# Projection matmuls given a scheduling offset of 200 in the first phase of a diffusion step on one core

## The chip, the core and the metric

The kernel runs on one core of one Trainium2 chip. The time is the device time of one execution in microseconds (us). The engines are TensorE (PE for its matmuls, PEld for its weight loads), VectorE (DVE), ScalarE (ACT), GpSimd (POOL) and SyncE (SP, which issues the DMAs). Each engine works through its own list of instructions in the order in which the program was built, and waits at an instruction whose inputs are not ready, even where a later one could run.

## The reference

One layer of a diffusion backbone is computed for a prompt of 128 tokens and a sample of 2048 tokens, model width 1024:

```
h = rmsnorm(x) * (1 + scale) + shift
p = h @ w_in                     # 1024 x 2832, one combined projection
A: gated DeltaNet (short conv on q/k/v, two scans in chunks of 64)
B: spatial gating MLP            C: average pooling minus identity
D: 2-D Fourier transform         each times silu(its gate columns of p)
out = x + gate * (concat(A, B, C, D) @ w_out);  y = rmsnorm(out)
```

All is float32. The outputs are y for the prompt and the sample and the prompt's final scan states.

## The kernel before

The 17 tiles of 128 tokens are worked on in three groups: group 0 has tiles 0 to 5, group 1 tiles 6 to 11, group 2 tiles 12 to 15 and the prompt's tile 16. The program has two phases.

**The first phase** is `phase_a`, called once for each group. For a group, `x_fin` transposes the normalised x on PE (L342, into the one PSUM buffer `pc`), ACT applies scale and shift (L344), and `h_split` writes the result as a high and a low half into `BIG` (L353 on DVE, L354 on DVE or POOL). All projections read these halves. The weights come in slices of 128 columns: `load_w` loads a slice by two DMAs (`wst`), ACT makes its high half (L242), DVE and POOL one part each of its low half (L243). There are three slots for slices. Then `mm3` makes one projection: 24 matmuls (8 slices of the contraction, three products of halves each) that add up in one of three PSUM buffers `pj`, all on L250. A slice of `w_in` is used for two chunks of tokens in the first phase, 384 and 392 wide in groups 0 and 1, 320 and 320 in group 2, so for 48 matmuls. The projections of the first phase are those of branch D with the beta and decay logits (272 columns), of C, and of q, k and v of two pairs of heads.

What follows on a projection in the first phase is a chain of small work: the short convolution (L842 on DVE), transposes back to token order (L642), the scalars of the decay (L562, L586, L587, L597), the products of k with k and of k with q (L673, L703), and, for a whole group, the `lanes`: transposes of the triangular blocks (L731), a solution in 30 steps, each a product and a sum on DVE (L741, L743), and its way back (L767, then L783, L784, L792 and L793). The records leave for DRAM. All these small matmuls are short, 10 to 64 columns or a 128x128 transpose.

**The second phase** begins after the third group (`Ring.late` is set to True): the gates' projections (L250 again, called by `gates`), branch B, the scan of 34 steps (L1053), the Fourier branch, and at the end the output projection of 17 tiles, 96 matmuls for every four column blocks.

**What sets the order.** The program is written in one sequence, and a scheduler then puts each engine's instructions in an order by a priority, which is the position in the sequence, among those that it takes to be ready. `hp(o)` opens a block whose instructions get a priority as if they stood o instructions earlier. The weight loads and `x_prep`, `x_fin` have 500 (`OW`, `OX`). The block in `mm3` has 0 (`OP`), so a projection competes by its own place in the sequence, behind all small matmuls written ahead of it:

```
def mm3(out, lh, rh, ks=range(KC), first=0, last=KC - 1):
    with hp(OP):
```

The engines' lists are fixed when the program is built; nothing is reordered at run time.

## Time and profile before

| | |
|---|---|
| median of 3 runs | 1208.77 us (1204.91 to 1215.5) |
| profiled execution | 1211.1 us, of it 1209.3 us from the first to the last instruction |
| mean granted TensorE clock | 0.952 |
| PE busy | 1090.1 us (90%) |
| PEld busy | 986.3 us (82%) |
| DVE busy | 815.1 us (67%) |
| POOL, ACT busy | 432.6 us (36%), 417.9 us (35%) |

The profile is of one execution. An engine counts as busy from the start to the modelled end of an instruction, so a busy PE is not a PE at its best rate. The clock column gives the share of 2.4 GHz that was granted to TensorE; it is 1.0 or 0.5 at any moment, and a mean in a longer stretch. In the trace, the 64-wide float32 products (L562, L586, L587, L673, L703, L767, L1053 and the like) appear as two matmuls for each one of the program; projections and transposes appear once.

### The profile page before, as it was taken

To read this page: it belongs to the slowest core of one execution; us is meant where nothing else is said; L and a number is where in the kernel's file an instruction comes from. 1 tells how busy PE (TensorE), PEld (TensorE's weight loads), DVE (VectorE), ACT (ScalarE), POOL (GpSimd) and SP (SyncE) were. 2 spreads that over 40 slices of the span, in tenths; PEclk is the share of its full clock that TensorE was granted. 3 is DMA by queue.
4 is the path that set the end of the run, shared out by engine and by line. 5 is a ranking of instruction groups with operands and counts; after the bars stand their busy time and mean duration, and the time that the engine had idled before them with its cause. 6 is when DMAs were issued, how large, how long until landed. Compare 5 with 4: busy or idle time off the path is not lost.

```text
span 1209.3 us, 29864 instructions
## 1 busy us (share of the span) xinstructions
PE 1090.1 (90%) x12211; PEld 986.3 (82%) x12211; DVE 815.1 (67%) x1864; ACT 417.9 (35%) x837; POOL 432.6 (36%) x429
## 2 busy tenths in 40 slices
PE   5888988998799698898979989898999889999997
PEld 2488977998779697875879888887899778999997
DVE  3666886799974699934884633784243488878665
ACT  2355667656565756123123111121111211111211
POOL 1347364726442237510231242232135343433212
PEclk9899998999879799898999999999999989999999
DMA  9879549943644564645264556589355645544331
GB/s 309 302 250 316 139 120 232 279 131 83 148 114 104 126 151 112 192 142 143 70 187 125 160 165 211 181 262 306 89 160 167 213 136 166 173 133 150 106 131 70
DMA packets 251391, 204.28 MB, mean 169 GB/s; under 512 B 109138, under 2 KB 218706, under 8 KB 250998
## 3 DMA queue, kind: packets, MB, share of 16 engines
q1 hardware_dynamic: 251254, 202.37, 56.7%
q8 instruction: 96, 1.57, 0.5%
q14 instruction: 41, 0.34, 0.1%
HBM read 138.86 MB, written 63.46 MB: 167 GB/s over the span
## 4 chain that ended last, share of the span: by engine, by line
PE 45%; DVE 17%; DMA 11%; issue 4%; ACT 3%; SPq 1%; POOL 1%; DVEq 0%; ACTq 0%; POOLq 0%
PE pj L250 34%; PE pa L1053 3%; DMA wst<-in_wt_dram 2%; DVE LL L743 2%; DVE ltmp L741 2%; DVE BIG L243 2%; DVE acc L842 1%; DMA X<-xd_d 1%; DMA ada<-in_ada_dram 1%; PE pb L1295 1%; DMA hr<-h_d 1%; DMA wos<-in_wo_dram 1%; DVE BIG L240 1%; DMA wst<-in_wv_dram 1%; PE pb L1393 1%
## 5 line engine op out<-in xcount | busy, mean ns | idle before, releaser
L250 PE MATMUL pj<-BIG 128*128 128x256 f32 (+4 forms) x3888 | 615.9, 313 | 16.7 <-ACT g L1222 4.0
L250 PEld LDWEIGHTS pj<-BIG 128*128 128x128 f32 x3888 | 560.9, 195 | 36.2 <-issue 10.8
L250 PE MATMUL pj<-BIG,yh 128*128 128x256 f32 x1088 | 197.5, 286 | 3.6 <-ACT BIG L1355 2.4
L243 POOL TENSOR_TENSOR BIG<-wst,BIG 128x512 fp32r<-128x512 f32 (+1 forms) x66 | 96.0, 1455 | 235.4 <-DVE BIG L240 137.3
L250 PEld LDWEIGHTS pj<-BIG,yh 128*128 128x128 f32 x1088 | 164.6, 190 | 7.0 <-ACT BIG L1355 2.6
L250 PE MATMUL pj<-BIG,yl 128*128 128x256 f32 x544 | 141.3, 284 | 0.0
L250 PEld LDWEIGHTS pj<-BIG,yl 128*128 128x128 f32 x544 | 98.7, 190 | 0.7
L240 DVE CAST BIG<-wst 128x512 fp32r<-128x512 f32 (+2 forms) x72 | 38.6, 540 | 74.8 <-DMA wst<-in_wt_dram 34.5
L1060 POOL TENSOR_TENSOR gS<-S,sc_s 128x256 f32<-128x256 f32 x32 | 20.9, 655 | 133.8 <-DVE S L1075 128.3
L842 DVE SCALAR_TENSOR_TENSOR acc<-raw,prm,acc 128x768 f32<-128x768 f32 (+1 forms) x72 | 64.2, 908 | 5.5 <-ACT acc L840 5.5
L1374 ACT ACTIVATE yh<-yt 128x768 fp32r<-128x768 f32 (+1 forms) x34 | 20.7, 629 | 128.9 <-issue 47.3
L1222 ACT ACTIVATE g<-pj 128x256 f32<-128x256 f32 (+1 forms) x64 | 23.3, 396 | 118.3 <-PE pj L250 111.8
L243 DVE TENSOR_TENSOR BIG<-wst,BIG 128x512 fp32r<-128x512 f32 (+1 forms) x66 | 53.4, 808 | 15.9 <-ACT BIG L242 13.8
L1413 POOL TENSOR_TENSOR z<-z,xs 128x1024 f32<-128x1024 f32 x16 | 41.8, 2612 | 57.1 <-DVE z L1405 52.0
L741 DVE TENSOR_TENSOR ltmp<-LL 128x60 f32<-128x60 f32 (+14 forms) x90 | 53.6, 595 | 4.5 <-ACT LL L734 3.1
L743 DVE TENSOR_TENSOR LL<-LL,ltmp 128x60 f32<-128x60 f32 (+14 forms) x90 | 55.3, 614 | 1.4
L242 ACT ACTIVATE BIG<-wst 128x512 fp32r<-128x512 f32 (+1 forms) x60 | 37.6, 632 | 35.3 <-DMA wst<-in_wt_dram 14.0
L354 POOL TENSOR_TENSOR BIG<-h,BIG 128x384 fp32r<-128x384 f32 (+2 forms) x28 | 26.7, 953 | 54.0 <-DVE BIG L353 37.4
L1075 DVE TENSOR_TENSOR S<-pa,gS 128x256 f32<-128x256 f32 x34 | 14.3, 420 | 42.1 <-PE pc L1053 35.0
L1375 DVE TENSOR_TENSOR yl<-yt,yh 128x768 fp32r<-128x768 f32 (+1 forms) x34 | 37.3, 1112 | 7.8 <-ACT yh L1374 7.8
L1405 DVE TENSOR_TENSOR z<-pj,gbc 128x256 f32<-128x256 f32 x68 | 26.0, 419 | 22.5 <-PE pj L250 22.2
L1071 ACT ACTIVATE xn<-pa 128x256 f32<-128x256 f32 x34 | 12.9, 381 | 80.8 <-PE pa L1053 73.2
(291 smaller groups left out, 1846.1 us busy)
## 6 DMA issues: line engine op xcount, KB each, us to landing
wst<-in_wt_dram SPq DMA_DIRECT2D x96, 256.0 KB, 3.5
R<-rec_d SPq DMA_DIRECT2D x136, 128.0 KB, 3.1
ada<-in_ada_dram SPq DMA_DIRECT2D x24, 512.0 KB, 5.3
C<-com_d SPq DMA_DIRECT2D x68, 128.0 KB, 3.1
xs<-xs_d SPq DMA_DIRECT2D x16, 512.0 KB
out_dram<-z SPq DMA_DIRECT2D x16, 512.0 KB, 3.1
x<-in_xs_dram SPq DMA_DIRECT2D x13, 512.0 KB
xs_d<-x SPq DMA_DIRECT2D x13, 512.0 KB, 6.1
```

What stands on the lines that cost most here:

```text
L240: nc.vector.tensor_copy(hi[:, ks, a:a + w], st[:, :, :w])
L242: nc.scalar.activation(hi[:, ks, a:a + w], st[:, :, :w], AF.Copy)
L243: (nc.vector if k0 == 0 else nc.gpsimd).tensor_tensor(lo[:, ks, a:a + w], st[:, :, :w], hi[:, ks, a:a + w].bitcast(F32), op=ALU.subtract)
L250: nc.tensor.matmul(out, lh[a](k), rh[b](k), start=(k == first and i == 0), stop=(k == last and i == 2))
L354: (nc.gpsimd if f % 2 else nc.vector).tensor_tensor(hT[1][:, f, off:off + w], h, hi.bitcast(F32), op=ALU.subtract)
L741: nc.vector.tensor_tensor(tv, X[:, :, j, j + 1:32].unsqueeze(2).to_broadcast([128, 2, j, ni]), bc(X[:, :, 0:j, j], ni), op=ALU.mult)
L743: nc.vector.tensor_tensor(X[:, :, 0:j, j + 1:32], X[:, :, 0:j, j + 1:32], tv, op=ALU.add)
L842: nc.vector.scalar_tensor_tensor(o, raw[:, si + j:si + j + n], w[:, j:j + 1], o, op0=ALU.mult, op1=ALU.add)
L1053: nc.tensor.matmul(ps[o, q], lh(q)[hp], rh[hp, q])
L1375: nc.vector.tensor_tensor(yl[:, q], yt[:, q], yh[:, q].bitcast(F32), op=ALU.subtract)
L1405: nc.vector.tensor_tensor(z[:, ns], ps, gbc[:, cd, ns], op=ALU.mult)
L1413: nc.gpsimd.tensor_tensor(z, z, xs, op=ALU.add)
```

## The change

The block in `mm3` gets 200 in the first phase, and 0 as before in the second. A projection matmul that the scheduler takes to be ready then goes ahead of any small matmul that is written up to 200 instructions ahead of it. The instructions themselves, the tiles, the buffers and the weight loads are the same; x_fin keeps its 500 and so stands ahead of the projections still.

```diff
-    OW, OX, OP = 500, 500, 0
+    OW, OX = 500, 500
...
     def mm3(out, lh, rh, ks=range(KC), first=0, last=KC - 1):
-        with hp(OP):
+        with hp(0 if Ring.late else 200):
```

Three places of PE's list show what moves. The first is in group 1, where the 48 products of k with k of one pair of heads stand (L673); `pj` is a projection, `pb` the PSUM buffers of the small matmuls. Before:

```order
L642 MATMUL pb<-cm,acc 128x128 x6
L250 MATMUL pj<-BIG 128x272 x105
L673 MATMUL pb<-sl 32x64 x48
L250 MATMUL pj<-BIG 128x384 x7
L250 MATMUL pj<-BIG 128x392
```

The same kind of products in the changed kernel, again in group 1:

```order
L673 MATMUL pb<-sl 32x64
L250 MATMUL pj<-BIG 128x392
L673 MATMUL pb<-sl 32x64 x23
L250 MATMUL pj<-BIG 128x384
L673 MATMUL pb<-sl 32x64
L250 MATMUL pj<-BIG 128x384
L673 MATMUL pb<-sl 32x64
L342 MATMUL pc<-cm,x 128x128
```

One closed block of 48 has become runs that alternate with single projection matmuls.

The second place is the beginning of group 2, while its x is still being transposed (L342). 272-column projections are the first of the group; 320-column ones are its chunks of C, q, k and v; L767 is the way back of the lanes of group 0. Before:

```order
L250 MATMUL pj<-BIG 128x272 x2
L767 MATMUL pa<-cm,LL 64x48 x9
L597 MATMUL pb<-cm,kt 24x128
L642 MATMUL pb<-cm,sl 128x128 x4
L250 MATMUL pj<-BIG 128x272 x3
L767 MATMUL pa<-cm,LL 64x48
L250 MATMUL pj<-BIG 128x272
L767 MATMUL pa<-cm,LL 64x48 x2
L342 MATMUL pc<-cm,x 128x128
L767 MATMUL pa<-cm,LL 64x48 x5
```

In the changed kernel:

```order
L250 MATMUL pj<-BIG 128x272 x2
L250 MATMUL pj<-BIG 128x320 x19
L342 MATMUL pc<-cm,x 128x128
L250 MATMUL pj<-BIG 128x320 x5
L250 MATMUL pj<-BIG 128x272 x7
L597 MATMUL pb<-cm,kt 24x128
L642 MATMUL pb<-cm,sl 128x128 x4
L250 MATMUL pj<-BIG 128x320 x6
L342 MATMUL pc<-cm,x 128x128
L250 MATMUL pj<-BIG 128x320 x3
L767 MATMUL pa<-cm,LL 64x48
```

The first 320-column projections stand here ahead of the lanes' way back; before, 96 of its matmuls (128 in all for a group) stood ahead of the first of them.

The third is the last place at which the two lists of PE differ, in the second phase, between the Fourier matmuls (L1195, L1196, L1183) and the scan (L1053):

```order
 L1195 MATMUL pb<-F,wcs 128x256
 L1196 MATMUL pb<-F,wcs 128x256
-L250 MATMUL pj<-BIG 128x256 x18
+L250 MATMUL pj<-BIG 128x256 x21
 L1053 MATMUL pa<-r,R 64x64 x8
 L1183 MATMUL pb<-tab,Z 128x256
```

Behind it the two lists are the same to the end.

## Rows read from the trace of the kernel before

**Rows 1.** The page: span, and busy time of the engines.

```profile
span 1209.3 us, 29864 instructions
PE 1090.1 (90%) x12211; PEld 986.3 (82%) x12211; DVE 815.1 (67%) x1864; ACT 417.9 (35%) x837; POOL 432.6 (36%) x429
```

**Rows 2.** Stages: stretch, length, PE, PEld, DVE, ACT, POOL busy, PEclk, DMA share, GB/s.

```profile
97.00:106.00 9.00, 9.00 (x55) 9.00 (x54) 4.76 (x6) 6.42 (x11) 8.85 (x10) 1.00 1.05 377
106.00:309.00 203.00, 181.58 (x1357) 169.82 (x1356) 175.19 (x314) 122.58 (x209) 107.32 (x105) 0.95 0.61 166
309.00:363.00 54.00, 47.92 (x612) 41.13 (x612) 46.01 (x112) 33.27 (x69) 25.38 (x32) 0.78 0.63 147
363.00:453.00 90.00, 79.70 (x1048) 73.38 (x1048) 60.56 (x143) 53.90 (x114) 27.41 (x37) 0.92 0.53 127
453.00:700.00 247.00, 220.21 (x2807) 196.23 (x2805) 171.46 (x347) 71.33 (x169) 69.74 (x77) 0.94 0.50 142
700.00:1209.30 509.30, 477.66 (x5910) 443.63 (x5903) 304.35 (x831) 93.30 (x200) 163.06 (x140) 0.98 0.53 166
```

**Rows 3.** PE's waits from 97 to 453 us: total, times, longest.

```profile
PE pc L342 <- DVE x L331: 6.3, 3, 5.2
PE pc L342 <- ACT h L344: 5.6, 7, 1.1
PE pb L642 <- ACT pt L599: 5.0, 1, 5.0
PE pb L642 <- ACT sl L844: 3.6, 2, 3.0
...
PE pj L250 <- ACT BIG L242: 1.9, 2, 0.9
...
PE pj L250 <- DVE BIG L243: 0.4, 1, 0.4
```

**Rows 4.** PE in order of time, group 0 (start, length, last: idle before).

```profile
106.04 8.92 PE L250 MATMUL pj<-BIG 128*128 128x392 f32 x49
120.13 0.47 PE L342 MATMUL pc<-cm,x 128*128 128x128 f32 x1 [5.17 <-DVE x L331]
...
124.81 4.49 PE L250 MATMUL pj<-BIG 128*128 128x384 f32 x24
```

**Rows 5.** PE in order of time, way back of the lanes, and first 320-column projection.

```profile
345.71 1.98 PE L767 MATMUL pa<-cm,LL 48*64 48x48 f32 x29
...
362.61 0.39 PE L250 MATMUL pj<-BIG 128*128 128x320 f32 x1
...
621.26 2.06 PE L767 MATMUL pa<-cm,LL 40*64 40x40 f32 x64
```

**Rows 6.** Two short stretches, columns as in rows 2.

```profile
250.00:300.00 50.00, 44.29 (x269) 41.96 (x269) 49.60 (x73) 30.30 (x50) 23.30 (x22) 0.97 0.42 104
...
341.00:358.00 17.00, 16.91 (x196) 15.07 (x194) 14.36 (x32) 8.87 (x22) 9.26 (x8) 0.51 0.67 151
```

**Rows 7.** PE in order of time where projections and products alternate.

```profile
574.12 22.09 PE L250 MATMUL pj<-BIG 128*128 128x320 f32 x153
598.19 1.22 PE L1276 MATMUL pb<-swt,v 128*64 128x128 f32 x10 [1.98 <-DVE v L1266]
599.35 0.56 PE L250 MATMUL pj<-BIG 128*128 128x320 f32 x2
...
600.20 0.56 PE L250 MATMUL pj<-BIG 128*128 128x320 f32 x2
```

**Rows 8.** DVE's part of the weight slices' low halves (L243), first to sixth.

```profile
94.80 0.69 DVE L243 TENSOR_TENSOR BIG<-wst,BIG 128x512 fp32r<-128x512 f32 x1 [2.87 <-ACT BIG L242]
...
143.57 0.69 DVE L243 TENSOR_TENSOR BIG<-wst,BIG 128x512 fp32r<-128x512 f32 x1 [0.24 <-ACT BIG L242]
```

**Rows 9.** DVE scales the last tile of x in the first phase.

```profile
346.62 1.66 DVE L331 TENSOR_SCALAR x<-x,rr 128x1024 f32<-128x1024 f32 x1
```

## The prediction, made before the changed kernel was run

> **What bounds the kernel now.** I began with the page's busy times [rows 1]: PE is busy in 1090 of 1209 us, DVE in 815. So the end is set by PE's work plus what PE loses, and PE's work is the same in both kernels. I then cut the span at the places that the order of the instructions gives. Up to about 97 us PE's list is unchanged. The last differing piece is among the scan and Fourier matmuls in the second phase; from about the 2600th projection matmul on, which the trace has at 700 us, both lists have the same number of every kind of matmul behind them. So the stretch from 700 us, 509 us long [rows 2], only shifts, and the whole effect is what PE loses between 97 and 700 us.
>
> The stage table [rows 2] gives the loss. From 97 to 453 us PE is busy 9.0 + 181.6 + 47.9 + 79.7 = 318.2 of 356 us: 37.8 us idle. From 453 to 700 us it is idle 247 - 220.2 = 26.8 us, but there new projections have the same priority as before. Why 453: the trace has the 1512th projection matmul there, and at that point both orders have finished all the same small matmuls but 5 transposes to token order and 20 products of k with q. Whatever the change wins or loses is won or lost before that point, and carried on.
>
> Now PE's waits in that stretch, which add up to the 37.8 us [rows 3]. Transposes of x wait 6.3 + 5.6 = 11.9 us, projections only 1.9 + 0.4 = 2.3 us, and the other small matmuls the rest, 23.6 us. So PE stands at small matmuls whose inputs come late, while projections are as good as never late. This is what the change acts on: a small matmul that stands farther behind its producer waits less.
>
> **The change part by part.** It adds and removes no instruction; each part is a matter of order.
>
> *Waits at small matmuls, 23.6 us.* At most all of it goes, at least none: where projections run out, PE waits as before. The starved place is 309 to 363 us, group 2's start, where PE loses 6.1 us idle [rows 2] and the last tile of x is only scaled at 346.6 us [rows 9]. I take half, 11.8 us.
>
> *The first transposes of group 1.* PE stands 5.17 us before 120.13 us at a transpose that waits for DVE [rows 4]. The changed list has 317 projection matmuls ahead of it and not 288. 29 more at 8.92 / 49 = 0.182 us are 5.3 us [rows 4], as long as the hole. Bounds 0 and 5.2; their weight slice may be a little late, so 3.5 us.
>
> *More changes between kinds of matmul.* Up to the 1512th projection matmul, PE's list changes 93 times between a projection and one of the short products (L562, L586, L587, L673, L703, L767 and those behind them) before, and 171 times after. The nearest price is at 599 us, where two projection and two short ones alternate: one round takes 600.20 - 599.35 = 0.85 us [rows 7]. Two projections alone take 2 x 22.09 / 153 = 0.29 us, two products 2 x 1.22 / 10 = 0.24 us [rows 7]; the other 0.32 us are two changes, 0.16 us each. 78 more cost 12.6 us where PE has no spare time, and nothing where it would have waited. I take half, 6.3 us lost.
>
> *The hole at group 2's start.* Before, PE fills it with L767, and the first 320-column projection comes at 362.6 us [rows 5]. After, 320-column projections go first and L767 later: the same work, changed about. The gain is in the clock. From 341 to 358 us PE is busy 16.91 of 17 us, with short matmuls mostly, and the granted clock is 0.51, almost all of it the 1.2 GHz level [rows 6]. L767 takes 1.98 / 29 = 0.068 us each there, and 2.06 / 64 = 0.032 us at 621 us [rows 5]. Bounds: nothing, and half of the 17 us, 8.5. I take 3 us, some 80 of L767's 256 matmuls in the trace.
>
> The Trainium skill (TensorE: Matmul & The Clock Gate, Part 1) says that the array's clock is throttled by default and released by activity. The trace agrees only if a busy share of 99% [rows 6] may still be little activity. By that rule projections among the short matmuls would give back all 8.5 us, and the sum would be 1198.
>
> *Projections put first that are not ready.* A weight slice serves 48 matmuls, two times 4.49 us [rows 4], so PE can use one up in 9.0 us. The halves on DVE from the first to the sixth come (143.57 - 94.80) / 5 = 9.8 us apart [rows 8]. Where projections always go first, PE may come to wait for slices, 0.8 us for each of the 24 slices (two of C and six of q, k and v for each group), 19 us in all. The lower bound is no new wait, since the waits shown are 2.3 us [rows 3]. I take 4 us, near that row, since slices are loaded with a priority of 500 and while PE does its transposes.
>
> *Later small work.* The lanes of group 0 come later against the projections, but DVE, which solves them, is full from 250 to 300 us (49.6 of 50 us [rows 6]) and has 90 - 60.6 = 29.4 us free from 363 to 453 us [rows 2]. Nobody needs their records before the scan, which starts at the same place among the projections. Cost nothing, and if that cover fails, group 1's lanes are late, whose solution on DVE comes next.
>
> Sum: 1211.1 (the profiled execution's own time, 2.3 us over the median of 1208.8, both inside the three runs' spread) - 11.8 - 3.5 + 6.3 - 3 + 4 = 1203.1 us.
>
> In place of the matmuls' busy time, PE's weight loads can be taken: 9.0 + 169.8 + 41.1 + 73.4 = 293.3 us of the 356 [rows 2], which would leave 62.7 us to be won, not 37.8. The Trainium skill (Trainium Kernel Development and Optimization, Performance Expectations) holds weight loads to be the better measure and a matmul's busy time a bad one; by it a full filling could reach 1211 - 63 = 1148 us. The trace speaks for the smaller sum: PE's named waits are the 37.8 us.
>
> **The rivals.** What a measurement of this kernel can tell from no change is about 1%, 12 us: faster is below 1196.7, slower above 1220.9.
>
> - *Forecast: filled in part and partly paid back*, 1203, from 1192 to 1213. Chance 0.42, of which 0.08 lies below 1196.7.
> - *Filled fully.* All 23.6 + 5.2 us of waits go, 6 us of slow clock too, and 6.3 are paid: 1211.1 - 28.5 = 1183, from 1174 to 1194. For it speaks that only 2.3 us of PE's waits are at projections and that DVE has room in all but one stretch. Against it: PE's waits are then someone else's lateness, and DVE's full 50 us do not get shorter. Chance 0.25.
> - *No difference, because others set the pace.* Group 1 is held by DVE from 250 to 300 us [rows 6], group 2's start by the chain of x, transpose, ACT and DVE; PE just waits at other instructions. 1209, from 1205 to 1213. Chance 0.13; a change that does nothing at all is excluded by the order.
> - *Slower: PE waits for weight slices.* The place is groups 0 to 2's q, k and v; the price 19 us for the slices and all 12.6 us for the changes of kind, against 15.3 us won: 1227. It decides where PE comes to want a slice sooner than every 9.8 us. For it speaks that these two paces, 9.0 and 9.8 us, are close. Chance 0.20.
>
> So faster is 0.25 + 0.08 = 0.33, within 1% 0.34 + 0.13 = 0.47, slower 0.20. The range from 1180 to 1228 leaves out the far parts of the second and the last case, about 0.09 each.
>
> **What would show it.** Right: PE's waits at L642, L562 and L673 from 97 us to the 1512th projection matmul fall from 23.6 to about 12 us, that matmul comes some 8 us sooner than 453 us, and the stretch behind the scan's first steps keeps its length. Waits at L250 for L242 and L243 stay under 8 us, and the L673 that stand alone among projections show gaps of about 0.16 us. Wrong: L250 waits for slices in tens of us, or the waits of L342 for ACT and DVE grow by what the others lose, or the lanes of group 1 and 2 become late so that PE idles between 500 and 700 us more than the 26.8 us of now.

## The result, and the profile after

The changed kernel is slower: 1249.87 us in the median of 4 runs (1248.03 to 1253.32) beside 1212.13 us for the kernel before in the same session, a ratio of 1.0318 with the interval [1.0251, 1.0385]. That is 38 us lost where the terms of the forecast add up to 8 us gained (1211.1 to 1203.1), and outside the range of 1180 to 1228 us.

The page of the changed kernel, span and busy times:

```profile
span 1246.1 us, 29876 instructions
PE 1121.5 (90%) x12211; PEld 1002.2 (80%) x12211; DVE 812.9 (65%) x1864; ACT 414.7 (33%) x835; POOL 437.4 (35%) x429
```

Against [rows 1] the span is 36.8 us longer, with the same 12211 matmuls. PE is busy 31.4 us longer (1121.5 - 1090.1), and what is left of the span when its busy time is taken off grows by 5.4 us (124.6 - 119.2). So most of the loss is not waiting, as this page counts it. It is the same matmuls taking longer, and the sum of the forecast had no place for that.

Next come the stages of the changed kernel, cut at its 816th, 1056th, 1512th and 2600th projection matmul (columns as in [rows 2]; the start, on which the two lists agree, came 4 us sooner in this execution, so the first cut is at 93 us and not at 97):

```profile
93.00:247.91 154.91, 139.49 (x928) 126.90 (x926) 103.57 (x188) 87.42 (x147) 86.00 (x84) 0.94 0.66 186
247.91:321.96 74.05, 73.25 (x454) 61.31 (x454) 53.74 (x99) 35.33 (x67) 22.75 (x25) 0.80 0.39 101
321.96:478.00 156.04, 132.38 (x1637) 116.07 (x1637) 118.22 (x274) 87.71 (x180) 66.31 (x76) 0.84 0.51 121
478.00:726.47 248.47, 221.74 (x2858) 197.73 (x2857) 174.33 (x355) 73.59 (x176) 69.95 (x77) 0.96 0.51 146
726.47:1246.10 519.63, 481.66 (x5903) 447.19 (x5901) 309.13 (x838) 93.37 (x200) 162.21 (x140) 0.96 0.52 163
```

The second and the third stage of the kernel before, between the same projection matmuls:

```profile
250.00:308.79 58.79, 51.74 (x314) 49.08 (x314) 58.39 (x91) 32.79 (x54) 26.78 (x24) 0.97 0.37 91
308.79:452.37 143.58, 127.20 (x1654) 114.06 (x1653) 106.15 (x254) 87.17 (x182) 53.00 (x70) 0.87 0.56 134
```

The loss sits in three places: 15.3 us in the second stage (74.05 - 58.79), 12.5 us in the third, and 10.8 us in the last one, from the 2600th projection on (519.6 against 508.8 us). In the second stage PE hardly waits any more, 0.8 us of 74 against 7.0 of 58.8, and still takes longer. Its granted clock is 0.80 there and not 0.97, and DVE, which was busy in 58.4 of 58.8 us, is idle for 20 us.

What PE does at the head of that stretch. In the kernel before, the 96 records of L673 for one pair stand together:

```profile
216.98 1.44 PE L673 MATMUL pb<-sl 64*32 64x64 f32 x96
```

In the changed kernel, PE in order of time:

```profile
245.24 0.30 PE L673 MATMUL pb<-sl 64*32 64x64 f32 x2 [1.44 <-ACT tm L721]
245.47 0.45 PE L250 MATMUL pj<-BIG 128*128 128x392 f32 x1
245.84 0.30 PE L673 MATMUL pb<-sl 64*32 64x64 f32 x2
...
256.48 0.42 PE L673 MATMUL pb<-sl 64*32 64x64 f32 x2
256.83 0.69 PE L250 MATMUL pj<-BIG 128*128 128x384 f32 x1
257.44 0.42 PE L673 MATMUL pb<-sl 64*32 64x64 f32 x2
257.79 0.69 PE L250 MATMUL pj<-BIG 128*128 128x384 f32 x1
...
270.90 1.65 PE L250 MATMUL pj<-BIG 128*128 128x384 f32 x4
```

Of the 48 products (two records each), 23 stand in one block and most of the others alternate with projections. A round of one projection and one product takes 0.96 us (256.83 to 257.79). At the prices of closed runs it would be 0.182 us [rows 4] and 1.44 x 2 / 96 = 0.03 us, 0.21 in all. From 245.24 to 270.90 us PE does 24 projections, the 96 records of L673 and 6 transposes: 25.7 us for what costs 4.4 + 1.4 us in closed runs and perhaps 1 us for the transposes. The granted clock falls to its lower level at 246.2 us and stays there for 30.7 us, in a stage in which PE waits 0.8 us in all. It falls 1 us after the first turn and the wait of 1.44 us ahead of it, so this place alone doesn't tell whether the wait or the turns brought it down; the experiments do. DVE's waits from 245.2 to 273 us have one entry; it stands at the end of this row of products:

```profile
DVE Ld L683 <- PE pb L673: 9.2, 1, 9.2
```

PE's waits of the changed kernel from 93 to 478 us, the answer to [rows 3]:

```profile
PE pj L250 <- DVE BIG L243: 6.4, 2, 3.6
PE pb L586 <- ACT acc L853: 5.2, 3, 3.5
...
PE pc L342 <- DVE x L331: 3.1, 3, 2.3
PE pj L250 <- ACT raw L823: 3.1, 2, 2.6
...
PE pc L342 <- ACT h L344: 2.1, 6, 0.6
PE pb L586 <- DVE S L633: 2.0, 1, 2.0
```

The waits on which the forecast counted did get shorter: the transposes of x fall from 11.9 to 3.1 + 2.1 = 5.2 us. But PE stands elsewhere instead, at projections (2.3 before, 10.5 now with the small rows) and at L586, and its whole idle time in this stretch goes from 37.8 to 39.9 us. At the small matmuls other than the transposes of x it is 39.9 - 5.2 - 10.5 = 24.2 us, and was 23.6. A third of PE's idle time stands at the beginning of group 2 (columns as in [rows 2]):

```profile
318.00:350.00 32.00, 19.06 (x181) 16.84 (x180) 32.00 (x54) 15.47 (x30) 22.50 (x19) 0.68 0.44 111
```

PE is idle there for 12.9 of 32 us, and DVE, which was idle while the products alternated, is busy in all of them. PE in order of time at the first transposes of group 1, the answer to [rows 4]:

```profile
113.27 1.68 PE L250 MATMUL pj<-BIG 128*128 128x384 f32 x8 [0.37 <-POOL raw L812]
117.72 1.51 PE L250 MATMUL pj<-BIG 128*128 128x384 f32 x7 [2.77 <-DVE BIG L243]
121.54 0.48 PE L342 MATMUL pc<-cm,x 128*128 128x128 f32 x1 [2.31 <-DVE x L331]
```

The one wait of 5.17 us has become three, of 5.45 us together, two of them at projections.

### The profile page after: what moved, and what is told of

Same layout as the page of the kernel before. It is cut to its first block, busy times and chain, and to the rows that moved or that the text cites. A ratio compares the mean times of both kernels' runs of the same rounds, so it can differ in the third digit from the quotient of the medians.

```text
span 1246.1 us, 29876 instructions
## 1 busy us (share of the span) xinstructions
PE 1121.5 (90%) x12211; PEld 1002.2 (80%) x12211; DVE 812.9 (65%) x1864; ACT 414.7 (33%) x835; POOL 437.4 (35%) x429
## 4 chain that ended last, share of the span: by engine, by line
PE 50%; DVE 15%; DMA 14%; ACT 6%; issue 4%; SPq 3%; POOL 2%; DVEq 0%; ACTq 0%; POOLq 0%
PE pj L250 38%; DMA wst<-in_wt_dram 4%; PE pa L1053 3%; DVE LL L743 1%; DMA Pf<-pf_d 1%; DMA yt<-y_d 1%; DMA R<-rec_d 1%; DVE ltmp L741 1%; DVE acc L889 1%; PE pb L673 1%; DVE rawc L897 1%; PE pb L1295 1%; SPq L1042 1%; DVE BIG L243 1%; PE pb L1393 1%
## 5 line engine op out<-in xcount | busy, mean ns | idle before, releaser
L250 PE MATMUL pj<-BIG 128*128 128x256 f32 (+4 forms) x3888 | 640.2, 319 | 25.7 <-DVE BIG L243 6.4
L250 PEld LDWEIGHTS pj<-BIG 128*128 128x128 f32 x3888 | 572.1, 198 | 49.9 <-issue 9.3
L250 PE MATMUL pj<-BIG,yh 128*128 128x256 f32 x1088 | 197.6, 286 | 2.9 <-ACT BIG L1355 1.9
L243 POOL TENSOR_TENSOR BIG<-wst,BIG 128x512 fp32r<-128x512 f32 (+1 forms) x66 | 92.2, 1398 | 247.6 <-DVE BIG L240 132.8
L250 PEld LDWEIGHTS pj<-BIG,yh 128*128 128x128 f32 x1088 | 164.6, 190 | 6.3 <-ACT BIG L1355 2.0
L250 PE MATMUL pj<-BIG,yl 128*128 128x256 f32 x544 | 141.3, 284 | 0.0
L250 PEld LDWEIGHTS pj<-BIG,yl 128*128 128x128 f32 x544 | 98.7, 190 | 0.7
L240 DVE CAST BIG<-wst 128x512 fp32r<-128x512 f32 (+2 forms) x72 | 37.8, 526 | 80.1 <-PE pj L250 40.0
L842 DVE SCALAR_TENSOR_TENSOR acc<-raw,prm,acc 128x768 f32<-128x768 f32 (+1 forms) x72 | 63.5, 896 | 13.2 <-ACT acc L840 13.1
L243 DVE TENSOR_TENSOR BIG<-wst,BIG 128x512 fp32r<-128x512 f32 (+1 forms) x66 | 54.8, 830 | 20.6 <-ACT BIG L242 17.4
L242 ACT ACTIVATE BIG<-wst 128x512 fp32r<-128x512 f32 (+1 forms) x60 | 37.5, 632 | 43.0 <-DMA wst<-in_wt_dram 19.8
L743 DVE TENSOR_TENSOR LL<-LL,ltmp 128x60 f32<-128x60 f32 (+14 forms) x90 | 50.5, 561 | 1.2
L354 POOL TENSOR_TENSOR BIG<-h,BIG 128x384 fp32r<-128x384 f32 (+2 forms) x28 | 31.2, 1114 | 46.4 <-DVE BIG L353 38.3
L1075 DVE TENSOR_TENSOR S<-pa,gS 128x256 f32<-128x256 f32 x34 | 14.3, 420 | 45.8 <-PE pc L1053 30.5
L1375 DVE TENSOR_TENSOR yl<-yt,yh 128x768 fp32r<-128x768 f32 (+1 forms) x34 | 36.8, 1098 | 8.1 <-ACT yh L1374 8.1
L344 ACT ACTIVATE h<-pc,modab 128x384 f32<-128x384 f32 (+2 forms) x44 | 26.0, 592 | 45.2 <-PE pc L342 38.7
```

What stands on the lines that cost most here:

```text
L240: nc.vector.tensor_copy(hi[:, ks, a:a + w], st[:, :, :w])
L242: nc.scalar.activation(hi[:, ks, a:a + w], st[:, :, :w], AF.Copy)
L243: (nc.vector if k0 == 0 else nc.gpsimd).tensor_tensor(lo[:, ks, a:a + w], st[:, :, :w], hi[:, ks, a:a + w].bitcast(F32), op=ALU.subtract)
L250: nc.tensor.matmul(out, lh[a](k), rh[b](k), start=(k == first and i == 0), stop=(k == last and i == 2))
L344: nc.scalar.activation(h[:, :w], ps[:, :w], AF.Identity, scale=modab[:, 0, f, cond:cond + 1], bias=modab[:, 1, f, cond:cond + 1])
L354: (nc.gpsimd if f % 2 else nc.vector).tensor_tensor(hT[1][:, f, off:off + w], h, hi.bitcast(F32), op=ALU.subtract)
```

## The experiments

Three theories stood at the start. **A**: single projections between single float32 products cost time, by each change from one kind to the other and by the clock that falls meanwhile. **B**: small work that is held back starves DVE first and then stands alone, without projections to fill the gaps. **C**: projections that come early wait for what they need (weight halves, the eviction of their PSUM buffer by ScalarE).

For A the number that counts is how often PE's order changes, up to the 2400th projection matmul, between a projection and one of the products of the first phase (L562, L586, L587, L673, L703, L767, L783, L784, L792, L793), and how many projections stand alone between two products. This table sorts the runs by it. PE busy and the rest of the span are of the one profiled execution, against 1090.1 and 119.2 us before. The last column is PE's busy time in the stretches in which the trace records the lower level of the clock, against 99.7 us before. Single executions scatter: the kernel before took 1201 to 1218 us over the sessions, so a few us in these three columns mean nothing, and the profiled execution of lanes up was 12 us above its median, that of -50 8 us below. A ratio is to the kernel before in the run's own session, and goes before a difference of two medians.

| run | changes (alone) | median us | ratio to before, interval | PE busy | rest | at half clock |
|---|---|---|---|---|---|---|
| offset 1000 | 72 (0) | 1289.88 | 1.0657 [1.0605, 1.071] | +25.9 | +53.2 | +57.9 |
| before, products raised 300 | 76 (1) | 1226.21 | 1.0112 [1.0055, 1.017] | +3.6 | +16.6 | +37.4 |
| products and lanes up | 100 (0) | 1228.41 | 1.0126 [1.0075, 1.0177] | +3.3 | +8.4 | +13.2 |
| -50, closed more | 104 (1) | 1221.85 | 1.01 [1.0061, 1.0139] | +4.7 | +8.5 | +15.9 |
| offset 100 | 116 (3) | 1227.38 | 1.0127 [1.008, 1.0174] | +1.6 | +14.8 | -2.0 |
| -50, closed | 120 (9) | 1221.56 | 1.011 [1.0065, 1.0154] | +1.9 | +5.4 | +9.9 |
| offset -100 | 120 (6) | 1209.64 | 0.9982 [0.995, 1.0015] | +4.8 | -0.2 | +19.0 |
| groups 0 and 2 only | 121 (0) | 1222.64 | 1.0096 [1.0057, 1.0135] | +2.2 | +8.8 | +13.7 |
| products up | 123 (9) | 1233.83 | 1.0185 [1.015, 1.0221] | +5.2 | +14.3 | +21.7 |
| **before** | 125 (7) | 1207 to 1213 | 1 | 0 | 0 | 0 |
| L673 up | 135 (17) | 1241.59 | 1.0267 [1.0213, 1.032] | +19.6 | +17.8 | +38.8 |
| products and evictions up | 145 (12) | 1224.21 | 1.0107 [1.0028, 1.0186] | +14.4 | -2.6 | +26.4 |
| products and transposes up | 157 (29) | 1235.28 | 1.0227 [1.0169, 1.0284] | +11.5 | +11.7 | +19.3 |
| before, L673 down | 159 (21) | 1231.83 | 1.0169 [1.0133, 1.0205] | +20.1 | +4.6 | +43.4 |
| offset -50 | 182 (30) | 1226.55 | 1.0127 [1.0073, 1.0182] | +23.2 | -15.7 | +30.5 |
| **changed (200)** | 205 (31) | 1249.87 | 1.0318 [1.0251, 1.0385] | +31.4 | +5.4 | +32.6 |
| group 1 only | 224 (44) | 1256.24 | 1.0396 [1.0347, 1.0446] | +38.0 | +11.3 | +54.5 |
| offset 150 | 256 (18) | 1254.85 | 1.0375 [1.0328, 1.0421] | +29.7 | +18.3 | +6.4 |
| lanes up | 262 (36) | 1257.75 | 1.0418 [1.0338, 1.0498] | +60.5 | -1.7 | +76.7 |

PE busy and the last column read together say more than the time. At the lower level the same work takes at most twice as long, so about half of the last column, by estimate, is time that the clock took. With that taken off PE busy, what is left goes with the number of changes: over the 19 kernels 0.17 us for each (correlation 0.93, against 0.80 for PE busy as it stands). For L673 up, L673 lowered and offset 1000 next to nothing is left, so there PE's longer busy time is the clock's. The clock is also low beside waits, so its part is not the alternation's alone.

**The price by itself.** A kernel of its own computes nothing of the reference: dense projections, then projections and products in turns of different lengths.

```diff
+    alt(0, 1, prod, 96)
+    warm()
+    alt(1, 1, prod, 96)
+    warm()
+    alt(2, 2, prod, 48)
...
```

> PE alone, on one chip run of its own: runs of 96 projections (384 columns, as L250) with stretches between them in which projections alternate with float32 products (64 rows, 32 by 64, as L673) one by one, 2 by 2, 4 by 4, 8 by 8, 24 by 24, and one by one with 128x128 transposes. It computes nothing of the reference. Theory A (the alternation costs the time): a one-by-one round takes about 0.47 us at the full clock and 0.97 us at the half clock, against 0.19 us for its two instructions in closed runs, and the granted clock falls to 0.5 within the one-by-one stretch, though PE counts as busy; at 24 by 24 nothing is lost; with transposes a round stays near 0.25 us. Theory B (the small work that comes late costs the time): the one-by-one round is at most 0.3 us and the clock stays at 1.0.

PE in order of time (L34 is a projection, L42 a product of 32x64): one by one at first, a little later, and then two by two.

```profile
44.24 0.45 PE L34 MATMUL p<-xr 128*128 128x384 f32 x1
44.62 0.30 PE L42 MATMUL q<-xb 64*32 64x64 f32 x2
44.84 0.44 PE L34 MATMUL p<-xr 128*128 128x384 f32 x1
...
51.02 0.69 PE L34 MATMUL p<-xr 128*128 128x384 f32 x1
51.64 0.42 PE L42 MATMUL q<-xb 64*32 64x64 f32 x2
51.99 0.69 PE L34 MATMUL p<-xr 128*128 128x384 f32 x1
...
151.42 0.62 PE L34 MATMUL p<-xr 128*128 128x384 f32 x2
151.97 0.30 PE L42 MATMUL q<-xb 64*32 64x64 f32 x4
152.20 0.62 PE L34 MATMUL p<-xr 128*128 128x384 f32 x2
```

And the stretches of the closed blocks, of one by one before and after the clock fell, of two by two, and of one by one with 128x128 transposes in place of the products (PE busy, PEld, ..., PEclk):

```profile
20.00:44.00 24.00, 24.00 (x313) 23.42 (x311) 0.00 (x0) 0.00 (x0) 0.00 (x0) 1.00 0.01 2
44.00:50.50 6.50, 6.50 (x34) 3.53 (x33) 0.00 (x0) 0.00 (x0) 0.00 (x0) 1.00 0.00 0
50.50:132.20 81.70, 81.70 (x255) 39.27 (x254) 0.00 (x0) 0.00 (x0) 0.00 (x0) 0.50 0.00 0
151.30:188.00 36.70, 36.70 (x287) 20.65 (x285) 0.00 (x0) 0.00 (x0) 0.00 (x0) 1.00 0.00 1
327.10:354.40 27.30, 27.30 (x193) 25.81 (x192) 0.00 (x0) 0.00 (x0) 0.00 (x0) 1.00 0.00 1
```

A round takes 0.60 us at the full clock (44.24 to 44.84) and 0.97 us at half of it (51.02 to 51.99). Projections in a closed run took 0.175 us here, from one start to the next, and products 0.03, so a round loses 0.39 us, 0.20 for each change, and 0.76 us once the clock has fallen. Theory A had 0.47 us for the first of the two rounds, too little, and 0.97 for the second. The clock falls although PE counts as busy in every microsecond. Two by two loses 0.37 us for each round of twice the work and keeps the full clock. Longer turns keep it too and lose 0.32, 0.31 and 0.26 us a round (4, 8 and 24 of each), so two changes never came for nothing. One by one with transposes a round takes 0.29 us at the full clock, which leaves 0.11 us for the transpose and two changes together: it is the turns with these products that cost, not every turn with something small, and transposes are rightly left out of the count. All this is one execution, with one shape of projection and one of product. The round of the changed kernel at 256.83 us is that of the lower clock.

**L673 raised too.**

```diff
-                        nc.tensor.matmul(ps[o, t * 64:t * 64 + 64].rearrange("p (b j) -> p b j", b=2), k2[:, b],
+                        with tc.high_priority(offset=200): nc.tensor.matmul(ps[o, t * 64:t * 64 + 64].rearrange("p (b j) -> p b j", b=2), k2[:, b],
```

> The changed kernel, with the products of k with k (L673) raised by 200 as well, so that they stand in closed runs again (changes between them and projections fall from 67 to 9), all else as late as in the changed kernel. Theory A: the 20 us of the stretch from 246 to 277 us come back, about 1228 us. Theory B: the other small work is late still, 1245 to 1255 us. Theory C (weight slices wait): 1245 to 1255 us.

1241.59 us, 2.7% over the kernel before and not 3.2: some 6 us come back, with intervals that overlap, and theory A alone does not hold, as it put 1228 us. 10 added changes go here with 19.6 us of PE's busy time, which is the clock's (38.8 us more at the lower level, 23.9 of one stretch beginning at 320.5 us with 10.0 us of waits in it). The rest of the span grows by 17.8 us, 12.6 us of waits for ScalarE's eviction L823 among it.

**Offset 1000** (in place of 200):

```diff
+        with hp(0 if Ring.late else 1000):
```

> The changed kernel with an offset of 1000 in place of 200: projections stand still farther ahead of the small work, but with fewer changes between projections and products (72; before 125, changed kernel 205, up to the 2400th projection matmul). Theory A: faster than the changed kernel, 1200 to 1225 us. Theory B: as the small work is later still, 1255 us or more. Theory C: 1250 us or more, as projections are asked for sooner.

1289.88 us, the slowest of all, with the fewest changes. PE's waits from 93 to 497 us:

```profile
PE pj L250 <- ACT raw L823: 23.2, 7, 8.4
```

Here theory C names the largest wait, 23.2 of the 53.2 us by which the rest of the span grows: projections wait for ScalarE to empty their buffer. The eviction kept its priority; that it stands behind small work which itself waits for PE is argued and not shown. PE's busy time grows as well, by 25.9 us at a mean granted clock of 0.914, without any added change; half of its 57.9 us more at the lower level is all of that. So there are two prices and not one.

**Offset 150:**

```diff
+        with hp(0 if Ring.late else 150):
```

> The changed kernel with an offset of 150: 256 changes between projections and products, more than the changed kernel's 205, and small work less late. Theory A: 1250 to 1275 us. Theory B: between the two kernels, 1220 to 1245 us. Theory C: 1225 to 1250 us.

1254.85 us, no better than 200. A smaller offset does not mean a smaller price: what matters is which sequences the shift lays on top of each other, and 150 makes 256 changes. Their 131 more go with 29.7 us of busy time and little of it at the lower level (+6.4), 0.23 us each.

**All five float32 products raised by 200 with the projections** (L562, L586, L587, L673, L703), each edited as L673 above, so that only transposes and lanes are passed:

```diff
+                with tc.high_priority(offset=200): nc.tensor.matmul(o, lh, gl[:, :, 4 * d:4 * d + 4])
...
+                    with tc.high_priority(offset=200): nc.tensor.matmul(ps[c2 * 64:c2 * 64 + 64, t * 64:t * 64 + 64], kT[hp, tk], qT[hp, tk])
```

> The changed kernel with the float32 products (L562, L586, L587, L673, L703) raised by 200 as well, so that projections pass only transposes, DVE-fed lanes and what hangs on them. PE's order then changes 123 times between a projection and a product up to the 2400th projection matmul (125 in the kernel before, 205 in the changed one), 9 projections stand alone between two products (7 and 31). Theory A (one-by-one alternation with products costs the time, by the changes of kind and by the clock that falls in them): 1209 to 1217 us. Theory B (small work held back starves VectorE first and comes in a lump later): most of the loss stays, 1232 to 1248 us, VectorE idle 90 us or more between the 240th and the 1512th projection matmul (65 before, 104 changed). Theory C (projections wait for weight halves and for ScalarE's evictions): waits at L250 of 10 to 25 us in that stretch and 1225 to 1235 us.

1233.83 us. PE's busy time is nearly that of before (+5.2), which gives back 26 us of the 31.4. In time it gives back less: 1.3 of the 3.2%, 16 us of 38. 22 us of loss stay, most of them in the rest of the span, which grows by 14.3 us here and by 5.4 in the changed kernel. So by this run the alternation is worth some 16 us, less than half of the loss, because waits that it had covered come out without it; something else goes with moving projections ahead.

**L673 alone lowered by 200 in the kernel before**, with the alternation as the purpose:

```diff
+                        with tc.high_priority(offset=-200): nc.tensor.matmul(ps[o, t * 64:t * 64 + 64].rearrange("p (b j) -> p b j", b=2), k2[:, b],
```

> The kernel before with L673 alone lowered by 200: the products of k with k alternate with projections, one by one, as in the changed kernel; nothing else gets another place. 159 changes between projections and products (125 before), 21 single projections (7). Theory A: the 34 added changes and the clock cost 10 to 20 us: 1220 to 1230 us, with single-projection rounds of 0.6 us at full clock or 0.97 us at half clock as in the first experiment. Theory B: only the products of k with k come later, so the lanes start a little later: 1209 to 1217 us.

1231.83 us, 1.7% or 20 us slower, as theory A put it but for 2 us; B had 1217 at most. PE's busy time grows by 20.1 us in the profiled execution, in which it is busy 43.4 us longer at the lower level. The alternation appears in other places too, since the order behind L673 shifts; PE in order of time at the way back of the lanes:

```profile
395.89 0.42 PE L250 MATMUL pj<-BIG 128*128 128x320 f32 x1
396.24 0.31 PE L767 MATMUL pa<-cm,X 48*64 48x48 f32 x2
396.48 0.41 PE L250 MATMUL pj<-BIG 128*128 128x320 f32 x1
...
403.09 0.63 PE L250 MATMUL pj<-BIG 128*128 128x320 f32 x1
403.65 0.45 PE L767 MATMUL pa<-cm,X 48*64 48x48 f32 x2
404.03 0.63 PE L250 MATMUL pj<-BIG 128*128 128x320 f32 x1
```

Rounds of 0.59 us, and after some of them 0.94 us, as in the kernel of its own. The clock falls here at 399.9 us, and PE's waits in the 7 us before that are 0.2 us in all.

**Offset -100:**

```diff
+        with hp(0 if Ring.late else -100):
```

> The changed kernel with -100 in the place of 200 in the first phase: small matmuls that are ready go ahead of projections written up to 100 instructions ahead of them, so projections are pure filler. 120 changes between projections and products, 6 single projections, as before. Theory A: as before, 1204 to 1214 us. Theory B (what counts is that small work is not held back): as before or faster, 1190 to 1209 us, with VectorE idle below 65 us between the 240th and the 1512th projection matmul.

1209.64 us, the same as before. Putting small work first gains nothing, so the strong form of B, that any earlier small work helps, falls.

**The 200 in groups 0 and 2 only, and in group 1 only** (`Ring.gi` is the group):

```diff
+        with hp(0 if Ring.late else (200, 0, 200)[Ring.gi]):
...
+        with hp(0 if Ring.late else (0, 200, 0)[Ring.gi]):
```

> The changed kernel with the 200 given in groups 0 and 2 only; group 1's projections keep 0. 121 changes between projections and products, no projection alone between two products. In the trace of the changed kernel about 15 us of the loss came between the 816th and the 1056th projection matmul (group 1) and 12 us from there to the 1512th (into group 2). Theory A: 1209 to 1215 us. Theory B: two of three groups still hold small work back, 1222 to 1238 us.

> The changed kernel with the 200 in group 1 only, the complement of the run with groups 0 and 2 (10 us slower than before). 224 changes between projections and products, 105 of them at the lanes' way back (L767), 44 projections alone between two products. If the losses add up, 27 us: 1236 to 1242 us. Theory A by the count of changes (99 more than before, against 80 more in the changed kernel): 1245 to 1255 us. Theory B, one group of three: 1215 to 1225 us.

1222.64 and 1256.24 us. Groups 0 and 2, without an added change, cost 1.0%, where A had nothing; that is within B's range. Group 1 alone costs as much as the whole change or more (the intervals overlap): with only its projections moved, 105 changes fall on L767. The losses do not add up; each order has its own changes, and PE's busy time goes with those.

**Products and transposes raised, lanes raised, products and evictions raised, products and lanes raised**, all in the changed kernel and edited like L673 above: with the products also L597 and L642; the lanes' six lines alone (L731, L767, L783, L784, L792, L793); with the products also the evictions (L823, L875 and branch D's copies); with the products also the lanes' lines. One line of each kind:

```diff
+            with tc.high_priority(offset=200): nc.tensor.transpose(ps[:, t * 128:t * 128 + 128], src[:, (a + t) * 128:(a + t) * 128 + 128], ident)
...
+                        with tc.high_priority(offset=200): nc.tensor.matmul(ps[cp, e * nu:e * nu + nu], X2[rows, e], ident[rows, rows])
...
+                    with tc.high_priority(offset=200): nc.scalar.activation(raw[:, lo + o:hi + o], ps[:, lo - a:hi - a], AF.Copy)
```

> The changed kernel with the float32 products and the transposes to token order (L562, L586, L587, L597, L642, L673, L703) raised by 200 as well, so that projections pass only the lanes' matmuls (L731, L767, L783, L784, L792, L793). With the products alone raised (L642 and L597 still passed) the loss against the kernel before was 22 us. Theory B (the chain of transposes, scalars and products is held back, so that the lanes and the scan start later): the loss goes to at most a third, 1210 to 1219 us, and the first product of the scan (L1053) starts within 10 us of the 667 us before. If the lanes' own delay carries the loss: 1225 to 1235 us. Theory A counts 157 changes between projections and products (125 before, 205 changed), the added ones at L792 and L793: 10 us, 1222 us.

> The changed kernel with the lanes' matmuls alone (L731, L767, L783, L784, L792, L793) raised by 200, so that projections pass the products and transposes of the pairs and not the lanes. PE's order then changes 262 times between projections and products, 135 of them at L673 (205 and 67 in the changed kernel). Theory A, with 34 us for the 80 changes that the change added: 1255 to 1275 us, PE busy longer by 45 us or more than before between its first projection and the scan. Theory B alone (what is late is the chain to the lanes): the changed kernel's time or a little less, 1235 to 1250 us.

> As the run with the float32 products raised (1234 us), and ScalarE's evictions of the projections (L823, L875, the copies of branch D) raised by 200 as well, so that they keep their place to the projections. Theory C (projections that came early wait for their eviction, and everything behind them on PE): 10 us of the 22 us go, 1218 to 1226 us, and the waits of L250 for L823 are gone. Theory B: the same time within 6 us, 1228 to 1240 us.

> The changed kernel with all float32 products and all matmuls of the lanes raised by 200, so that projections pass the transposes (L597, L642) alone. 100 changes, no single projection. Where the products alone were raised, 22 us stayed, where products and transposes were raised, 27 us. If the lanes that are passed carry what stayed: 1203 to 1213 us. If the transposes (the chain to the scalars and the records) carry it: 1220 to 1232 us.

1235.28, 1257.75, 1224.21 and 1228.41 us. The second is A's strongest case: 262 changes, PE busy 60.5 us longer in an execution 12 us above the median, the rest of the span no longer than before. Its clock falls at 356.5 us, after turns of one and one and of two and two, with no wait in the 7 us before, and stays down for 27.3 us in which PE is always busy. The first and the fourth were to find the part of the small work that carries the 22 us of the run with the products raised, and together they do not: with transposes raised the loss is no smaller (2.3% against 1.9), which speaks against the transposes; with lanes raised it is 1.3%, within the range that stood for the transposes and far from the 1203 to 1213 us that stood for the lanes. The third is 0.8% nearer to before than with the products alone, with intervals that overlap; it lies in C's range, but waits of PE at L250 for L823 were 0.4 us with the products alone and are 1.3 us here, so the saving isn't the wait that C named.

**The two prices apart: offset 100 and offset -50.**

```diff
+        with hp(0 if Ring.late else 100):
...
+        with hp(0 if Ring.late else -50):
```

> The changed kernel with 100 in the place of 200: 116 changes between projections and products (125 before, 205 with 200, 256 with 150) and 3 single projections. Theory A (each change added costs about 0.4 us, the clock included): 1205 to 1213 us, though the edit points the same way as the one with 150, which was 45 us slower. Theory B (small work held back, by half as much): half of the 22 us that stayed when the products were raised, and half of the rest: 1218 to 1230 us.

> The changed kernel with -50 in the place of 200: small work goes ahead of projections, none is held back, but the shift meets the products of the lanes' way back and of k with k, so that they alternate: 182 changes between projections and products, 30 single projections (125 and 7 before; 120 and 6 with -100, which made no difference). Theory A: 57 added changes at 0.4 us, 1228 to 1238 us, PE busy longer by 20 us or so and not idle longer. Theory B: 1200 to 1212 us.

1227.38 and 1226.55 us, the same loss by opposite ways; the first lies in B's range, the second 1.5 us below A's. The page of offset 100, then that of -50:

```profile
span 1225.7 us, 29858 instructions
PE 1091.7 (89%) x12211; PEld 986.8 (81%) x12211; DVE 817.7 (67%) x1864; ACT 423.3 (35%) x841; POOL 434.1 (35%) x429
```

```profile
span 1216.8 us, 29870 instructions
PE 1113.3 (91%) x12211; PEld 1005.8 (83%) x12211; DVE 814.5 (67%) x1864; ACT 415.5 (34%) x836; POOL 433.5 (36%) x429
```

With 100 PE is busy as before (+1.6) and idle 14.8 us longer: projections ahead of small work, with hardly an alternation, do not shorten the waits at all. With -50 nothing is held back, and PE is busy 23.2 us longer with 57 changes more, 0.4 us each, the clock included; 15.7 us of that come out of waits in this execution, the fastest of six. It also shows what brings the clock down: from 381.96 us projections and products of L767 take turns, nearly all one by one, PE never waits, and at 388.0 us the clock falls.

**Products in closed blocks in the kernel before**, all products and lanes' lines raised by 300:

```diff
+                        with tc.high_priority(offset=300): nc.tensor.matmul(ps[cp, e * nu:e * nu + nu], X2[rows, e], ident[rows, rows])
...
```

> The kernel before (offset 0) with all float32 products and the lanes' matmuls raised by 300: the reverse of the change, with the products in closed blocks, 76 changes between projections and products (125 before) and 1 single projection (7). Theory A: 49 changes fewer at 0.2 to 0.4 us: 1190 to 1202 us, faster than before. If the alternations that are left in the kernel before lie where PE waits anyway, or if products that stand too early make PE wait: 1206 to 1225 us.

1226.21 us: no gain from 49 changes fewer. This run also tests another explanation of the whole, that late lanes make the scan late. First and last product of the scan, before, changed, and here:

```profile
L1053 PE MATMUL pa<-S,C x544: 218/218/366, 666.7 to 1078.1; 64*64 64x64 f32 x182
```

```profile
L1053 PE MATMUL pa<-S,C x544: 218/218/363, 695.4 to 1115.0; 64*64 64x64 f32 x182
```

```profile
L1053 PE MATMUL pa<-S,C x544: 217/218/366, 629.2 to 1061.8; 64*64 64x64 f32 x182
```

In the changed kernel the scan starts 28.7 us later; here it starts 37.5 us sooner, and the kernel still ends later than before. So a later start of the scan is not by itself what ends the kernel later.

**-50 with L673 and L767 raised by 100, and by 200**, to close the two lines that alternate there:

```diff
+        with hp(0 if Ring.late else -50):
...
+                        with tc.high_priority(offset=100): nc.tensor.matmul(ps[cp, e * nu:e * nu + nu], X2[rows, e], ident[rows, rows])
```

> The run with offset -50 had PE idle 16 us shorter than before and busy 28 us longer. Here the two lines that alternated in it, L673 and L767, are raised by 100 besides, so that their blocks close: 120 changes between projections and products, 9 single projections (182 and 30 with -50 alone; 125 and 7 before). Theory A (the busy time is the price of alternation, and the shorter idle time stays): 1196 to 1207 us, faster than before. If the shorter idle time was only filled by the longer alternations: 1207 to 1216 us, no difference from before, as with -100.

> As the run before this one with 200 in the place of 100 for L673 and L767: 104 changes, 1 single projection. Theory A: 1192 to 1205 us. If the idle time depends on the order's distance from that of the kernel before more than on the changes, as in the run with products raised by 300 (idle 16 us longer): 1210 to 1228 us.

1221.56 and 1221.85 us, where theory A had 1207 at most. The busy time came back (+1.9 and +4.7; the 28 us of the expectation are 23.2 by the page above) and so did the waits (+5.4 and +8.5): as far as one execution of each tells, the 15.7 us of shorter waits with -50 were only filled by the longer alternation. No version here beats the kernel before.

## Why the prediction was wrong, by its steps

- **More changes between kinds of matmul, +6.3 us: the step that failed, with the premise under it that PE's work is the same in both kernels.** The count held (93 and 171 changes up to the 1512th projection in the two traces, as forecast). The price of a change at full clock nearly held too: 0.20 us in the kernel of its own against 0.16. 80 of them would be 16 us. Two things were missed. The alternation itself brings the clock down, so that a round then loses 0.76 us and not 0.39: PE was busy at the lower level for 132.3 us and not 99.7. A round took 1.6 times as long there (0.97 against 0.60 us) and plain work at most twice, so 12 to 16 us of the growth are the clock's, by estimate, which leaves some 15 to 19 for the changes. And half of the price was taken to fall where PE waits anyway; the place where most of it fell, 245 to 271 us, had only 7.0 us of waits to cover it. PE's busy time grew by 31.4 us. With L673 alternating in the kernel before it grew by 20.1, with 262 changes by 60.5; without added changes (offset 100, groups 0 and 2, products raised) by at most 5.2, offset 1000 with its long waits aside. In time the alternation is worth 16 us taken out (products raised) and 20 us put in (L673 lowered), of 38.
- **Waits at small matmuls, -11.8 us, and the first transposes of group 1, -3.5 us: failed as well.** The transposes of x gained 6.7 us and the projections lost 8.2; the waits at the other small matmuls stayed, 24.2 us against 23.6. At 120 us the 5.17 us of [rows 4] turned into 5.45 us: the 29 projections ahead came too early for their slice. Over the stretch PE's idle time is 2 us longer, and with 100, where hardly any alternation hides anything, the rest of the span is 14.8 us longer. A wait of PE at a small matmul was, as the second rival's counter-argument had it, someone else's lateness.
- **The signs named for being wrong** all looked at waits, and none of them showed: waits at L250 are 10.5 us and not tens, those of L342 fell, and from 478 to 726 us PE is idle for 26.7 us (26.8 before). No sign looked at PE's busy time.
- **Which measure of PE to trust.** The prediction kept to the matmuls' busy time against weight loads, which the Trainium skill (Trainium Kernel Development and Optimization, Performance Expectations) prefers. For this loss the trace agrees with the skill: in the one-by-one turns of the kernel of its own PE counts as busy in all of 81.70 us and loads weights in 39.27, against 23.42 of 24.00 in closed blocks. A loss inside PE's busy time can't appear in a sum of its waits.
- **Later small work, nothing.** The cover named for it was free time of DVE behind 363 us. DVE lost its time earlier: in the second stage, where it had been full [rows 6], it is idle 20 us, 9.2 of them at one instruction behind L673. Between the 240th and the 1512th projection its idle time, summed over its records, goes from 65 to 104 us. At group 2's start, from 318 to 350 us, it is then busy in all 32 us while PE is idle for 12.9. That the first is the reason of the second fits, and no run here takes the one away without the other.
- **Clock at group 2's start, -3 us.** It didn't come: the third stage's clock is 0.84 against 0.87, with 20.5 us at half from 324.7 us on. By the rule of the Trainium skill that was weighed there (TensorE: Matmul & The Clock Gate, Part 1), by which activity releases the clock, the prediction had projections among short matmuls give it back. Where they alternated one by one, the traces show the reverse: it stayed at half for 30.7 us, with a PE that hardly waited.
- **Projections put first that are not ready, +4 us.** Right in kind: 2.3 to 10.5 us, of which the slices are 6.7. The rival that forecast slower had the sign and not the mechanism: slices cost a third of its 19 us, and its 12.6 us for changes became 31.4 us of PE's busy time, the clock included.
- **The stretch from the 2600th projection, only shifted.** It was 10.8 us longer in this one execution. In the profiles of the other 18 kernels of the table it took 504.8 to 525.2 us, in no order that follows the number of changes. What makes it vary stays open; the kernel before itself varies by 17 us from execution to execution.
- **Open as well**: that seven of the eight orders with at most 125 changes, offset 1000 left aside, cost 1.0 to 1.9%, and one nothing. Their loss is mostly idle time of PE, at other instructions in each, and in part the clock. Raising transposes, lanes or evictions did not find one carrier, so of some 20 of the 38 us the runs show only that PE waits, at many places, and not what carries it.

## What to carry to other kernels

When a priority offset moves one sequence of matmuls, look first at where its shifted places fall on another sequence: the scheduler can merge the two one by one. Price a change by a row of a long alternation and not of a few rounds, 0.20 us here, and a long row of one and one at the lower clock. Compare offsets by the number of changes that the order shows, not by their size: 100, 150, 200 and 1000 gave 1.3, 3.8, 3.2 and 6.6%. The number tells PE's busy time and not its waits: offset 100 and offset -100 have 116 and 120 changes, and cost 1.3% and nothing. And a wait at an engine's small instruction is gained only if its producer gets sooner; putting other work ahead of it moves the producer's next input too.

## What the runs showed of the hardware that was not expected

A PE that counts as busy can bring its own clock down and hold it there: with a 128x384 projection and a 32-column float32 product in turn, PE busy in 81.70 of 81.70 us, the granted clock fell 6.5 us after the turns began and stayed at 0.50 until the next dense projections. In the kernel with offset -50 it fell 6.0 us after such turns began, also without a wait. Turns of two and two, and one projection with one 128x128 transpose, were busy throughout as well and kept 1.00 in the kernel of its own. A change between projection and product took about 0.20 us at the full clock, more than a whole projection in a closed run (0.175 us).
